# Six more landing places for the first weights, one modulation run per block, and three changes of order in a two-layer diffusion kernel

## The chip, the cores and the metric

The kernel runs on one core of a Trainium2 chip. The metric is the device time of one execution in microseconds (us), lower is better. TensorE is called PE here, VectorE DVE, ScalarE ACT, GpSimd POOL and SyncE SP; "PEld" is the loading of a matmul's stationary operand, which overlaps PE.

## The reference

Everything is float32: 256 latent tokens and 256 context tokens of width 2048, batch 1, two layers.

```
for i in range(2):
    shift, scale, gate = split(silu(c) @ ada_w[i] + ada_b[i], 3)
    h = rms_norm(x, norm_g[i]) * (1 + scale) + shift
    if i == 0:                                  # attention heads beside a state-space scan
        hc = the same of ctx, with the modulation vector c_ctx
        p, pc = h @ w_in, hc @ w_in             # q, gate, z, k, v, x/B/C, dt
        ya = neighbourhood_attention(norm(q), norm(k), v, norm(kc), vc, rpb) * silu(gate)
        yb = group_norm(bidirectional_ssd(conv(x,B,C), dt, ctx state) + d*x, silu(z))
        y = concat(ya, yb) @ w_out
    else:                                       # gated short convolution
        bg, cg, hv, g = split(h @ w_in, 4)
        y = (silu(g) * bg * conv3(cg * hv)) @ w_out
    x = x + gate * y
```

## The kernel before, in words

**Matmuls.** Each matrix product is made of three matmuls. A weight block of 128 x 1024 numbers arrives by DMA in a buffer called `raw`; ACT casts it to a rounded format (`wH`, line 414), DVE subtracts to get the remainder (`wL`, line 421), and the activations are split in the same way into `hH` (line 742) and `hL` (line 748). PE then sums hH·wH, hL·wH and hH·wL in a PSUM bank. Every such matmul is issued by the helper at line 189, every transposition by the one at line 193. There are eight PSUM banks, five `raw` buffers and three places for a split weight (`WH`, `WL`). Four tiles that have no work yet at the start (`PT0`, `PT1`, `xtm`, `yi`) serve as further `raw` buffers until `later_loads` takes them back.

**The first stage.** The first 160 us or so go through the 2048 input channels in eight blocks of 256, because the normalised input becomes ready block by block. In each block j, `ada_gen` computes scale (A0) and shift (S0) of the block for the latent and the context stream at once: 16 matmuls for each of the two parts, each using 32 of the 128 columns of the array (operand `cpad`), an ACT copy of the result (`half`, line 712), two transpositions and a short DVE reduction (lines 720 to 726). Then ACT and DVE make `hH` and `hL` of the two 128-channel halves. The main loop over j multiplies the block by the weights of K and V (four row groups t of 128 tokens, six matmuls each, each into a bank of its own, which DVE then adds into a running sum in SBUF, line 774: `sz` and `gt` hold K, `Vt` holds V), by those of Q (two row groups, in two fixed banks) and by a narrow block for the state-space part (`b_part`, two fixed banks). So four banks are left to turn over among the K and V parts and the modulation.

**Order.** The instruction order of all engines is written out by a planner at build time. `Plan` keeps a clock for each engine, with a cost for each instruction and a DMA rate (`RATE`). Tasks are generators that yield the engine and the operands that they wait for; `pump` lets a task issue when the planner's clocks say that it would not wait long, `force` issues whatever can go first until a condition holds. `urgent`, `side` and `back` are three queues of tasks in falling priority. On the chip each engine runs its list in order, so an instruction that waits holds back all behind it on its engine. The loads of weights go out on SP in one list, each when a buffer has become free.

```
def used():
    pos["use"] += 1
    free_w.append(in_use.popleft())
    splits_try()
```

A weight's place is given back by `used`, and then the next landed weight may be cast into it. In block one, K, V and Q are held together and given back after the last row group.

**Later stages.** Attention heads and state-space groups run as side tasks beside the remaining projections of the first layer. The vectors that gate the two residuals are a matrix-vector product on DVE (`gemv_gen`, line 802), spread in the background over all that time, fed by loads of `in_ada_w`. In the last projection of V (`v_gen`, line 996) two of the four copies out of PSUM go to DVE and two to ACT. The matmuls with `mix` that follow are the first layer's output projection; then come the second layer's input and output projections. The last one writes four column groups n; for each, `fin_gen` multiplies both halves of rows by the gate (line 1945), adds the residual (line 1947) and sends the result out (line 1949). Within a weight chunk the two halves of rows t alternate.

Of the kernel before, what the change touches and what calls it, by code (L numbers as in the profile page):

```python
# [9 lines left out]
F32R = mybir.dt.float32r  # L10
# [27 lines left out]
class Plan:  # L38


    NAMES = {"PE": "PE", "DVE": "DVE", "Activation": "ACT", "Pool": "POOL", "SP": "SP"}
    RATE = 270.0

    def __init__(self):
        self.t = dict.fromkeys(("PE", "DVE", "ACT", "POOL", "SP"), 0.0)
# [4 lines left out]
    def keys(self, ap):  # L50
        a, n = ap.ap, ap.tensor.name
        if type(ap.tensor).__name__ == "Tile" and not n.startswith("dram"):
            lo = ap.offset % a[0][0] if a[0][0] else ap.offset
            hi = lo + sum(abs(s) * (c - 1) for s, c in a[1:])
            return [(n, u) for u in range(lo // 128, hi // 128 + 1)]
        if n.startswith("in_") or n.startswith("out_"):
            return []
        hi = ap.offset + sum(abs(s) * (c - 1) for s, c in a)
        return [(n, u) for u in range(ap.offset // 256, hi // 256 + 1)]
# [82 lines left out]
def kernel(ctx: ExitStack, tc, x, cx, ada0, ada_w, ada_b, w_in, w_out, sc_in, sc_out, rpb, small, const,  # L142
# [12 lines left out]
    def st(shape, tag, dt=F32, name=None):  # L155
        return sb.tile(list(shape), dt, tag=tag, name=name or tag, bufs=1)
# [10 lines left out]
    WH = [st([128, 1024], f"wH{k}", F32R) for k in range(NW)]  # L167
    WL = [st([128, 1024], f"wL{k}", F32R) for k in range(NW)]

    KT, QT, Vt, gt = st([128, 4, 512], "KT", F32R), st([128, 4, 256], "QT", F32R), st([128, 4, 512], "Vt"), st([128, 4, 256], "gt")  # L170
    KL, QL = st([128, 4, 512], "KL", F32R), st([128, 4, 256], "QL", F32R)
    sz, xtm, yi = st([128, 4, 256], "sz"), st([128, 2, 512], "xtm"), st([128, 4, 256], "yi")
    PT = [st([128, 4, 256], f"PT{k}") for k in range(2)]

    spare = [t.rearrange("p a b -> p (a b)") for t in (PT[0], PT[1], xtm, yi)]
    free_r += spare
    spare_names = {t.tensor.name for t in spare}

# [151 lines left out]
    def bank():  # L330
        return take(free_b)
# [138 lines left out]

    def used():
        pos["use"] += 1
        free_w.append(in_use.popleft())
        splits_try()


# [16 lines left out]

    def later_loads():
        started[0] = True
        free_r[:] = [a for a in free_r if a.tensor.name not in spare_names]
        for n in range(16):
            lay = 0 if n < 4 else 1
            c0 = 4096 + n * 512 if n < 4 else (n - 4) * 512
            for k in range(8):  # L500
                later.append(("g", ("gem", n, k), ada_w[lay], k * 256, 2, c0, 512))
# [183 lines left out]

    A0 = st([128, KB, 2], "A0")
    S0 = st([128, KB, 2], "S0")
    g0 = P_("g0")

    def ada_gen():  # L690
        bc = lambda ap: ap.unsqueeze(2).to_broadcast([128, 2, 2])
        for j in range(8):
            k2 = slice(2 * j, 2 * j + 2)
            for part, dst in ((0, A0), (1, S0)):
                ps = None
                for q in range(4):
                    key = ("ada", j, part, q)
                    w_ = 2 if j == 0 else 4
                    if q % w_ == 0:
                        ks = [("ada", j, part, q + i) for i in range(w_)]  # L700
                        yield when(lambda: all(k in RAW for k in ks))
                        yield W_("PE", *[RAW[k][1] for k in ks], nb=0 if ps is not None else 1)
                    if ps is None:
                        ps = bank()
                    raw, v = RAW.pop(key)
                    for g in range(4):
                        mm(ps[32 * g:32 * g + 32, :256], cpad[:, 4 * q + g, :], v[:, g, :], q == 0, q == 3)
                    give_raw(raw)
                    issue()
                yield W_("ACT", ps)  # L710
                Rt = half()
                E(S.copy(Rt, ps[:, :256]))

                yield W_("PE", Rt)
                for b in range(2):
                    turn(ps[:, 256 + b * 128:384 + b * 128], Rt[:, b * 128:(b + 1) * 128])
                give(free_h, Rt)
                yield W_("DVE", ps)
                p2 = dst[:, k2, :]
                E(V.tensor_reduce(out=p2, in_=ps[:, 256:].rearrange("p (b g c) -> p b c g", b=2, c=32)[:, :, 0:2, :],  # L720
                                  axis=AX.X, op=ALU.add))
                if part == 0:
                    E(V.tensor_tensor(out=dst[:, k2, :], in0=p2, in1=bc(bs1[:, k2]), op=ALU.add))
                    E(V.tensor_tensor(out=dst[:, k2, :], in0=dst[:, k2, :], in1=bc(g0[:, k2]), op=ALU.mult))
                else:
                    E(V.tensor_tensor(out=dst[:, k2, :], in0=p2, in1=bc(P_("ab0")[:, k2]), op=ALU.add))
                give(free_b, ps)

            for ts in ((0, 1), (2,), (3,)) if j == 0 else ((0, 1, 2, 3),):
                yield when(lambda: all(("xm", t, j) in got for t in ts))  # L730
                spans = [(k, slice(max(256 * k, 128 * ts[0]), min(256 * k + 256, 128 * ts[-1] + 128)))
                         for k in range(2) if {2 * k, 2 * k + 1} & set(ts)]
                o = slice(128 * ts[0], 128 * ts[-1] + 128)
                for kb in (2 * j, 2 * j + 1):
                    yield W_("DVE", xnT[kb][:, o])
                    hf = tmp()
                    if hH[kb] is None:
                        hH[kb] = st([128, 512], f"hH{kb}", F32R, name=f"hH{kb}")
                    if ts == (0, 1):
                        split_half(kb)  # L740
                    for k, ok_ in spans:
                        E(S.activation(hH[kb][:, ok_], xnT[kb][:, ok_], AF.Identity, scale=A0[:, kb, k:k + 1],  # L742
                                       bias=S0[:, kb, k:k + 1]))
                        E(V.tensor_scalar(out=hf[:, ok_], in0=xnT[kb][:, ok_], scalar1=A0[:, kb, k:k + 1],  # L744
                                          scalar2=S0[:, kb, k:k + 1], op0=ALU.mult, op1=ALU.add))
                    if hL[kb] is None:
                        hL[kb] = st([128, 512], f"hL{kb}", F32R, name=f"hL{kb}")
                    E(V.tensor_tensor(out=hL[kb][:, o], in0=hf[:, o], in1=hH[kb][:, o].bitcast(F32), op=ALU.subtract))  # L748
                    give(free_t, hf)
                    if ts == (0, 1):  # L750
                        halfsplit.pop()()
                if ts == (0, 1):
                    hold[0] = False
                    split()
                    split()
                got.update(("h", j, t) for t in ts)
# [102 lines left out]
        used()  # L859

    for j in range(8):
        force(lambda: ("h", j, 0 if j == 0 else 3) in got, (urgent,))
        if j == 0:

# [14 lines left out]
                rows_(j, "Q", t, psQ[t], w3[2], True, False)  # L879
            for t in range(2, 4):  # L880
                force(lambda: ("h", j, t) in got, (urgent,))
                for key, k in (("K", 0), ("V", 1)):
                    kv(j, key, t, w3[k])
            for k in range(3):
# [3 lines left out]
        else:  # L888
# [7 lines left out]
                used()  # L896
            b_part(j)
    force(lambda: all(("part", 7, key, t) in got for key in "KV" for t in range(4)), (urgent,))
    got.add(("V", 0))


# [615 lines left out]
    def do_gv(a, nxt):  # L1517
        do_g(a, 4)
        psV = banks(4)
        proj(512, "act", psV, nxt, a == 3)  # L1520
        spawn(urgent, v_gen(a, psV))

    for a in range(1, 3):
        do_qk(a, 2)
# [410 lines left out]
    def fin_gen(n, ps):  # L1935
        cols = slice(n * 512, (n + 1) * 512)
        yield when(lambda: n_back[0] >= 15)
        gb, o = tmp(), tmp()
        yield W_("SP", mrow[3:4])
        E(DMA.dma_start(gb, mrow[3, cols].partition_broadcast(128)))  # L1940
        for t in range(2):
            if t:
                o = tmp()
            yield W_("DVE", ps[t], gb)
            E(V.tensor_tensor(out=o, in0=ps[t], in1=gb, op=ALU.mult))
            give(free_b, ps[t])
            E(V.tensor_tensor(out=o, in0=o, in1=x1[t][:, cols], op=ALU.add))
            yield W_("SP", o)
            E(DMA.dma_start(out[t * 128:(t + 1) * 128, cols], o))
            give(free_t, o)  # L1950
        give(free_t, gb)

    for n in range(4):
        if n == 1:
            force(lambda: n_back[0] >= 15, (urgent, back))
        ps = banks(2)
        for kb in range(0, KB, 2):
            force(lambda: y2[kb + 1] is not None)
            chunk(kb, "act", ps, kb == 0, kb == KB - 2, lambda i: (y2[i][:, 0], y2[i][:, 1]))
        spawn(urgent, fin_gen(n, ps), 3)  # L1960
    force(lambda: not urgent, (urgent,))


# [54 lines left out]
```

## Time and profile before

| | before |
|---|---|
| median of 3 runs (lowest to highest) | 1783.97 us (1783.84 to 1785.52) |
| the profiled execution's own time | 1784.02 us |
| its span in the profile | 1782.2 us |
| PE busy | 1755.5 us (99%), 9577 records |
| DVE / ACT / POOL busy | 71% / 43% / 2% of the span |
| mean DMA rate | 210 GB/s |

The profiled execution took 1784.02 us, of which 1.8 us lie outside the span. Matmuls are pipelined, so a matmul's busy time runs into the next one's; how fast PE issues is seen from the starts of neighbouring rows. PE's clock was granted in full throughout.

### The profile page before, as it was taken

How to read it: one execution, taken by the hardware profiler on the slowest of the kernel's cores; microseconds unless marked ns; L12 is line 12 of the kernel's file. 1: busy time of each engine (PE TensorE's matmuls, PEld its weight loads, DVE VectorE, ACT ScalarE, POOL GpSimd, SP SyncE). 2: the span in 40 equal slices, each digit the busy share in tenths (PEclk: the TensorE clock that was granted, in tenths of full speed). 3: DMA queues.
4: the chain of work that ended last, by engine and by line, in shares of the span. 5: the costliest groups of instructions: out<-in, count | busy, mean ns of one | idle time of the engine just before them, and what ended most of it. 6: DMA issues, size and time to landing. Idle time of an engine off the chain costs nothing.

```text
span 1782.2 us, 25428 instructions
## 1 busy us (share of the span) xinstructions
PE 1755.5 (99%) x9577; PEld 1470.5 (83%) x9577; DVE 1265.6 (71%) x1986; ACT 773.7 (43%) x1330; POOL 32.2 (2%) x28
## 2 busy tenths in 40 slices
PE   6999999999999999999999999999999999999998
PEld 4677888888888889888988898788888888888887
DVE  5666787878675878675887687787768777555554
ACT  5423544445242446242445443664546444444432
POOL 0000100001000000000001000000000000000000
PEclk9999999999999999999999999999999999999999
DMA  9987654666745666655675457658867787666563
GB/s 354 345 284 246 213 153 130 192 193 209 226 132 186 199 193 206 208 153 172 187 233 141 149 178 249 208 166 293 283 225 248 241 260 251 208 190 190 191 209 116
DMA packets 222363, 374.60 MB, mean 210 GB/s; under 512 B 32432, under 2 KB 69136, under 8 KB 222240
## 3 DMA queue, kind: packets, MB, share of 16 engines
q1 hardware_dynamic: 214928, 366.38, 63.9%
q10 hardware_dynamic: 7312, 6.61, 1.1%
q8 instruction: 75, 1.23, 0.3%
q14 instruction: 48, 0.39, 0.1%
HBM read 367.52 MB, written 6.72 MB: 210 GB/s over the span
## 4 chain that ended last, share of the span: by engine, by line
PE 93%; DMA 3%; DVE 2%; ACT 1%; issue 0%; POOL 0%; SPq 0%; ACTq 0%; DVEq 0%
PE bank L189 90%; PE bank L193 3%; DMA tmp<-dram_csr 1%; DVE wL L421 1%; DMA raw<-in_ada 0%; DMA tmp<-dram_exr 0%; DVE mix L1546 0%; DMA tmp<-dram_mixd 0%; DMA const<-in_const 0%; ACT wH L414 0%; DVE tmp L744 0%; DMA raw<-in_w_out 0%; DVE tmp L1388 0%; DVE hL L748 0%; DVE tmp L1399 0%
## 5 line engine op out<-in xcount | busy, mean ns | idle before, releaser
L414 ACT CAST wH<-raw 128x1024 fp32r<-128x1024 f32 (+1 forms) x375 | 390.8, 1044 | 595.0 <-PE bank L189 515.9
L421 DVE TENSOR_TENSOR wL<-raw,wH 128x1024 fp32r<-128x1024 f32 (+1 forms) x374 | 452.2, 1212 | 214.3 <-ACT wH L414 212.4
L189 PE MATMUL bank<-hH,wH 128*128 128x256 f32 (+1 forms) x1040 | 343.3, 330 | 0.8 <-ACT wH L414 0.8
L189 PE MATMUL bank<-hL,wH 128*128 128x256 f32 (+1 forms) x1040 | 338.0, 325 | 0.0
L189 PE MATMUL bank<-hH,wL 128*128 128x256 f32 (+1 forms) x1024 | 330.7, 323 | 0.9 <-DVE wL L421 0.9
L189 PE MATMUL bank<-wH,hH 128*128 128x512 f32 x640 | 257.1, 402 | 3.9 <-ACT hH L742 2.6
L189 PE MATMUL bank<-wL,hH 128*128 128x512 f32 x640 | 250.4, 392 | 0.0
L189 PE MATMUL bank<-wH,hL 128*128 128x512 f32 x640 | 249.8, 391 | 0.1
L802 DVE SCALAR_TENSOR_TENSOR acc<-raw,csil,acc 128x512 f32<-128x512 f32 x256 | 191.8, 749 | 65.2 <-DMA raw<-in_ada_w 56.0
L189 PE MATMUL bank<-wH,h 128*128 128x512 f32 x680 | 215.6, 391 | 0.0
L189 PEld LDWEIGHTS bank<-hH,wH 128*128 128x128 f32 x1040 | 196.5, 189 | 18.6 <-ACT wH L414 1.3
L189 PEld LDWEIGHTS bank<-hL,wH 128*128 128x128 f32 x1040 | 196.8, 189 | 15.5
L189 PEld LDWEIGHTS bank<-hH,wL 128*128 128x128 f32 x1024 | 194.0, 189 | 18.2 <-DVE wL L421 1.6
L189 PEld LDWEIGHTS bank<-wH,h 128*128 128x128 f32 x680 | 127.7, 188 | 26.5 <-issue 0.2
L189 PEld LDWEIGHTS bank<-wH,hH 128*128 128x128 f32 x640 | 120.2, 188 | 33.7 <-issue 5.0
L189 PEld LDWEIGHTS bank<-wH,hL 128*128 128x128 f32 x640 | 120.2, 188 | 26.1 <-DVE hL L748 0.6
L189 PEld LDWEIGHTS bank<-wL,hH 128*128 128x128 f32 x640 | 120.2, 188 | 24.7 <-DVE wL L437 0.5
L189 PE MATMUL bank<-wH,mix 128*128 128x512 f32 x432 | 138.8, 393 | 1.1 <-DVE Vt L996 1.1
L189 PE MATMUL bank<-wL,h 128*128 128x512 f32 x340 | 132.3, 389 | 0.0
L189 PEld LDWEIGHTS bank<-wH,mix 128*128 128x128 f32 x432 | 81.1, 188 | 18.7 <-DVE Vt L996 1.5
L189 PE MATMUL bank<-wL,mix 128*128 128x512 f32 x216 | 84.4, 391 | 0.3 <-DVE wL L421 0.3
L189 PEld LDWEIGHTS bank<-wL,h 128*128 128x128 f32 x340 | 63.9, 188 | 12.9
(284 smaller groups left out, 2173.9 us busy)
## 6 DMA issues: line engine op xcount, KB each, us to landing
raw<-in_w_in SPq DMA_DIRECT2D x208, 512.0 KB
raw<-in_ada_w SPq DMA_DIRECT2D x128, 512.0 KB
raw<-in_sc_in SPq DMA_DIRECT2D x128, 512.0 KB
raw<-in_w_out SPq DMA_DIRECT2D x64, 512.0 KB
raw<-in_ada SPq DMA_DIRECT2D x37, 512.0 KB
raw<-in_sc_out SPq DMA_DIRECT2D x32, 512.0 KB
tmp<-dram_csr SPq DMA_DIRECT2D x32, 256.0 KB
PT<-in_ada SPq DMA_DIRECT2D x14, 512.0 KB
```

Of the source, the lines that this page charges most:

```text
L189: E(T.matmul(o, l, r, start=start, stop=stop, skip_group_check=True))
L193: E(T.transpose(o, i, ident if k == 128 else ident[:k, :k]))
L414: E(S.copy(H, v))
L421: E(V.tensor_tensor(out=Lo, in0=v, in1=H.bitcast(F32), op=ALU.subtract))
L802: E(V.scalar_tensor_tensor(out=acc, in0=v[:, j], scalar=csil[:, 2 * k + j:2 * k + j + 1], in1=acc, op0=ALU.mult, op1=ALU.add))
```

## The change

The instructions that compute weights' products stay the same. The change has these parts:

1. QT, QL, KT and KL, which are written only after the first stage, lend their space: six more `raw` places until `later_loads`. Their real tiles are allocated after the stage.
2. For blocks four to eight (j > 2) scale and shift are computed in one run: 32 matmuls into one bank, one ACT copy of 128 x 512, four transpositions, one reduction of 128 x 8 into AS, three small operations.
3. For those blocks the making of `hH`/`hL` waits, for each half, until the main loop has reached the block or the planner's DVE clock is at most 600 ns ahead of PE's.
4. In block one Q's place is given back when only the last row group of K and V is left, so that the next weight is cast there earlier.
5. `v_gen` goes to the front of the urgent queue.
6. In the last column group the last six 128-channel blocks are done for the first half of rows, then for the second, and `fin_gen` waits for each half's marker before it takes that half's bank.
7. The planner: RATE is 310 in the first stage and 270 from `later_loads` on, and dependences on `small` and `const` are kept at a granularity of 2 columns instead of 128. These change no instruction, only the order that the planner chooses.

```
-    RATE = 270.0
+    RATE = 310.0
...
+            g = 2 if n[:5] in ("small", "const") else 128
+            return [(n, u) for u in range(lo // g, hi // g + 1)]
...
-    spare = [t.rearrange("p a b -> p (a b)") for t in (PT[0], PT[1], xtm, yi)]
+    spare = [t.rearrange("p a b -> p (a b)") for t in (PT[0], PT[1], xtm, yi)] + \
+        [st([128, 1024], n, name=f"first{n}") for n in ("QT", "QL")]
+    for n in ("KT", "KL"):
+        kt = st([128, 2, 1024], n, name=f"first{n}")
+        spare += [kt[:, 0], kt[:, 1]]
...
+        w = in_use.popleft()
+        if w is not None:
+            free_w.append(w)
...
     def later_loads():
         started[0] = True
+        plan.RATE = 270.0
...
+            if j > 2:
+                ks = [("ada", j, part, q) for part in range(2) for q in range(4)]
+                yield when(lambda: all(k in RAW for k in ks))
+                yield W_("PE", *[RAW[k][1] for k in ks], nb=1)
+                ps = bank()
+                for _, _, part, q in ks:
+                    raw, v = RAW.pop(("ada", j, part, q))
                     for g in range(4):
+                        mm(ps[32 * g:32 * g + 32, part * 256:part * 256 + 256], cpad[:, 4 * q + g, :], v[:, g, :],
+                           q == 0 and part == 0, q == 3)
...
+                Rt = tmp()
+                E(S.copy(Rt, ps))
...
+                for b in range(4):
+                    turn(ps[:, b * 128:(b + 1) * 128], Rt[:, b * 128:(b + 1) * 128])
...
+                E(V.tensor_reduce(out=AS, in_=ps.rearrange("p (b g c) -> p b c g", b=4, c=32)[:, :, 0:2, :], axis=AX.X, op=ALU.add))
+                E(V.tensor_tensor(out=A0[:, k2, :], in0=AS[:, 0:2], in1=bc(bs1[:, k2]), op=ALU.add))
+                E(V.tensor_tensor(out=A0[:, k2, :], in0=A0[:, k2, :], in1=bc(g0[:, k2]), op=ALU.mult))
+                E(V.tensor_tensor(out=S0[:, k2, :], in0=AS[:, 2:4], in1=bc(P_("ab0")[:, k2]), op=ALU.add))
...
                 for kb in (2 * j, 2 * j + 1):
+                    if j > 2:
+                        yield when(lambda: need[0] >= j or plan.t["DVE"] <= plan.t["PE"] + 600)
...
     for j in range(8):
+        need[0] = j
...
                 force(lambda: ("h", j, t) in got, (urgent,))
+                if t == 3:
+                    free_w.append(in_use[2])
+                    in_use[2] = None
+                    splits_try()
...
-        spawn(urgent, v_gen(a, psV))
+        urgent.insert(0, Task(v_gen(a, psV)))
...
+            yield when(lambda: n < 3 or (3, t) in at)
             yield W_("DVE", ps[t], gb)
             E(V.tensor_tensor(out=o, in0=ps[t], in1=gb, op=ALU.mult))
...
-        for kb in range(0, KB, 2):
+        for kb in range(0, KB if n < 3 else KB - 6, 2):
...
+    ws = [use(q) for q in range(3)]
+    for t in range(2):
+        for q, (H, Lo) in enumerate(ws):
+            for b in range(2):
+                hl = y2[KB - 6 + 2 * q + b]
+                for a_, w_ in ((0, H), (0, Lo), (1, H)):
+                    mm(ps[t], hl[:, a_, t * 128:(t + 1) * 128], w_[:, b], False, q == 2 and b == 1 and a_ == 1)
+                pump()
+        at.append((3, t))
+        pump()
```

More of the change, by code (lines that the diff above doesn't have):

```diff
@@ L54, in keys @@
             hi = lo + sum(abs(s) * (c - 1) for s, c in a[1:])
-            return [(n, u) for u in range(lo // 128, hi // 128 + 1)]
+            g = 2 if n[:5] in ("small", "const") else 128
+            return [(n, u) for u in range(lo // g, hi // g + 1)]
         if n.startswith("in_") or n.startswith("out_"):
@@ L168 @@
     WL = [st([128, 1024], f"wL{k}", F32R) for k in range(NW)]
-    KT, QT, Vt, gt = st([128, 4, 512], "KT", F32R), st([128, 4, 256], "QT", F32R), st([128, 4, 512], "Vt"), st([128, 4, 256], "gt")
-    KL, QL = st([128, 4, 512], "KL", F32R), st([128, 4, 256], "QL", F32R)
+    Vt, gt = st([128, 4, 512], "Vt"), st([128, 4, 256], "gt")
     sz, xtm, yi = st([128, 4, 256], "sz"), st([128, 2, 512], "xtm"), st([128, 4, 256], "yi")
     PT = [st([128, 4, 256], f"PT{k}") for k in range(2)]
-    spare = [t.rearrange("p a b -> p (a b)") for t in (PT[0], PT[1], xtm, yi)]
+    spare = [t.rearrange("p a b -> p (a b)") for t in (PT[0], PT[1], xtm, yi)] + \
[3 more added lines that the diff above has]
+        spare += [kt[:, 0], kt[:, 1]]
     free_r += spare
@@ L472, in used @@
         pos["use"] += 1
-        free_w.append(in_use.popleft())
+        w = in_use.popleft()
+        if w is not None:
+            free_w.append(w)
         splits_try()
@@ L687 @@
     S0 = st([128, KB, 2], "S0")
+    AS = st([128, 4, 2], "AS")
     g0 = P_("g0")
+    need = [0]
     def ada_gen():
@@ L693, in ada_gen @@
             k2 = slice(2 * j, 2 * j + 2)
[L694 to L705, printed above, removed]
+            if j > 2:
[5 more added lines that the diff above has]
+                    raw, v = RAW.pop(("ada", j, part, q))
                     for g in range(4):
-                        mm(ps[32 * g:32 * g + 32, :256], cpad[:, 4 * q + g, :], v[:, g, :], q == 0, q == 3)
+                        mm(ps[32 * g:32 * g + 32, part * 256:part * 256 + 256], cpad[:, 4 * q + g, :], v[:, g, :],
+                           q == 0 and part == 0, q == 3)
                     give_raw(raw)
@@ L710, in ada_gen @@
                 yield W_("ACT", ps)
-                Rt = half()
-                E(S.copy(Rt, ps[:, :256]))
+                Rt = tmp()
+                E(S.copy(Rt, ps))
                 yield W_("PE", Rt)
-                for b in range(2):
-                    turn(ps[:, 256 + b * 128:384 + b * 128], Rt[:, b * 128:(b + 1) * 128])
-                give(free_h, Rt)
+                for b in range(4):
+                    turn(ps[:, b * 128:(b + 1) * 128], Rt[:, b * 128:(b + 1) * 128])
+                give(free_t, Rt)
@@ L718, in ada_gen @@
                 yield W_("DVE", ps)
[L719 to L726, printed above, removed]
@@ L727, in ada_gen @@
-                give(free_b, ps)
+                E(V.tensor_reduce(out=AS, in_=ps.rearrange("p (b g c) -> p b c g", b=4, c=32)[:, :, 0:2, :], axis=AX.X, op=ALU.add))
+                E(V.tensor_tensor(out=A0[:, k2, :], in0=AS[:, 0:2], in1=bc(bs1[:, k2]), op=ALU.add))
+                E(V.tensor_tensor(out=A0[:, k2, :], in0=A0[:, k2, :], in1=bc(g0[:, k2]), op=ALU.mult))
+                E(V.tensor_tensor(out=S0[:, k2, :], in0=AS[:, 2:4], in1=bc(P_("ab0")[:, k2]), op=ALU.add))
+                give(free_b, ps)
+            else:
+                for part, dst in ((0, A0), (1, S0)):
+                    ps = None
+                    for q in range(4):
+                        key = ("ada", j, part, q)
+                        w_ = 4 if j else 2
+                        if q % w_ == 0:
+                            ks = [("ada", j, part, q + i) for i in range(w_)]
+                            yield when(lambda: all(k in RAW for k in ks))
+                            yield W_("PE", *[RAW[k][1] for k in ks], nb=0 if ps is not None else 1)
+                        if ps is None:
+                            ps = bank()
+                        raw, v = RAW.pop(key)
+                        for g in range(4):
+                            mm(ps[32 * g:32 * g + 32, :256], cpad[:, 4 * q + g, :], v[:, g, :], q == 0, q == 3)
+                        give_raw(raw)
+                        issue()
+                    yield W_("ACT", ps)
+                    Rt = half()
+                    E(S.copy(Rt, ps[:, :256]))
+                    yield W_("PE", Rt)
+                    for b in range(2):
+                        turn(ps[:, 256 + b * 128:384 + b * 128], Rt[:, b * 128:(b + 1) * 128])
+                    give(free_h, Rt)
+                    yield W_("DVE", ps)
+                    p2 = dst[:, k2, :]
+                    E(V.tensor_reduce(out=p2, in_=ps[:, 256:].rearrange("p (b g c) -> p b c g", b=2, c=32)[:, :, 0:2, :],
+                                      axis=AX.X, op=ALU.add))
+                    if part == 0:
+                        E(V.tensor_tensor(out=dst[:, k2, :], in0=p2, in1=bc(bs1[:, k2]), op=ALU.add))
+                        E(V.tensor_tensor(out=dst[:, k2, :], in0=dst[:, k2, :], in1=bc(g0[:, k2]), op=ALU.mult))
+                    else:
+                        E(V.tensor_tensor(out=dst[:, k2, :], in0=p2, in1=bc(P_("ab0")[:, k2]), op=ALU.add))
+                    give(free_b, ps)
@@ L898 @@
     force(lambda: all(("part", 7, key, t) in got for key in "KV" for t in range(4)), (urgent,))
+    KT, QT, KL, QL = st([128, 4, 512], "KT", F32R), st([128, 4, 256], "QT", F32R), st([128, 4, 512], "KL", F32R), st([128, 4, 256], "QL", F32R)
     got.add(("V", 0))
@@ L1960 @@
         spawn(urgent, fin_gen(n, ps), 3)
+    ws = [use(q) for q in range(3)]
+    for t in range(2):
+        for q, (H, Lo) in enumerate(ws):
+            for b in range(2):
+                hl = y2[KB - 6 + 2 * q + b]
[4 more added lines that the diff above has]
+        pump()
     force(lambda: not urgent, (urgent,))
```

## The prediction, on record before the changed kernel ran

> **What bounds the kernel now.** I read the page's busy line and the chain's shares first, then the list of what PE waited for, to see how much there is to win at all.
>
> ```profile
> span 1782.2 us, 25428 instructions
> PE 1755.5 (99%) x9577; PEld 1470.5 (83%) x9577; DVE 1265.6 (71%) x1986; ACT 773.7 (43%) x1330; POOL 32.2 (2%) x28
> PE 93%; DMA 3%; DVE 2%; ACT 1%; issue 0%; POOL 0%; SPq 0%; ACTq 0%; DVEq 0%
> PE bank L189 <- DMA raw<-in_ada: 11.9, 1, 11.9
> PE bank L189 <- ACT hH L742: 2.6, 2, 1.4
> PE bank L189 <- DVE wL L421: 1.2, 3, 0.7
> PE bank L189 <- DVE Vt L996: 1.1, 1, 1.1
> PE bank L189 <- DVE sz L774: 1.0, 1, 1.0
> PE bank L193 <- ACT half L712: 1.0, 2, 0.5
> PE bank L189 <- ACT wH L414: 0.8, 1, 0.8
> PE bank L189 <- DVE half L1433: 0.5, 1, 0.5
> PE bank L189 <- DVE tmp L1404: 0.4, 1, 0.4
> ```
>
> The columns of the last nine rows are the total wait in us, how often, and the longest. PE is busy for 99% of the span and carries 93% of the chain that ended last. The nine rows sum to 20.5 us, of which 11.9 is the one wait for the first loads, which nothing in the change shortens. So all waits that the change could remove come to 8.6 us, and everything that DVE or ACT saves counts only where it stands in one of these rows. What else can be won is PE's own work (the modulation runs) and the tail behind the last matmul. I make the sum against the profiled execution's own time, 1784.02 us (span 1782.2 and 1.8 around it), which is 0.05 above the median, so the same sum holds for the median. A measurement of this kernel can tell about 0.2%, 3.57 us, from no change.
>
> **The change part by part.**
>
> One modulation run for scale and shift, five blocks. This is one of the runs of a later block, on PE's timeline (start, duration, operation):
>
> ```profile
> 79.03 0.39 PE L189 MATMUL bank<-wL,hH 128*128 128x512 f32 x1
> 79.35 1.07 PE L189 MATMUL bank<-raw,cpad 128*32 128x256 f32 x16
> 80.24 1.05 PE L189 MATMUL bank<-PT,cpad 128*32 128x256 f32 x16
> 81.22 0.50 PE L189 MATMUL bank<-wH,hH 128*128 128x512 f32 x1
> 81.55 0.39 PE L189 MATMUL bank<-wH,hL 128*128 128x512 f32 x1
> 82.01 0.38 PE L193 MATMUL bank<-const,half 128*128 128x128 f32 x2
> 82.15 0.48 PE L189 MATMUL bank<-wH,hH 128*128 128x512 f32 x1
> 82.46 0.39 PE L189 MATMUL bank<-wH,hL 128*128 128x512 f32 x1
> ```
>
> A plain 128x512 matmul follows its neighbour by 0.23 (82.69 would be next after 82.46; 81.55 + 2 x 0.23 is 82.01). Each of the program's matmuls with `cpad` stands as two records, so the 16 of one part are these 32, in two halves of 0.89 (79.35 to 80.24) and 0.98 to the next operation. From 79.03 to 81.55 there are 2.52, of which two plain steps are 0.46: one part's run costs 2.06. Entering and leaving the 32-column form is 2.06 - 2 x 0.89 = 0.28 of that. A merged run has four halves and pays this once: 3.84 instead of 4.12, so 0.28 less in each of five blocks: **-1.4**. The transpositions: a pair takes 82.46 - 82.01 - 0.23 = 0.22, two pairs 0.44; four in a row cost between 0.22 and 0.44, so the gain is 0 to 0.22 per block; I take 0, the upper price, because each transposition still has its own issue (all five: 0 to -1.1). ACT makes one copy of 512 columns instead of two of 256 and DVE three small operations fewer in a block; PE waits for neither there (the wait for `half` line 712, 1.0 in all, is two of 0.5, in the first block, which keeps two runs): 0. A merged run starts when eight landed blocks lie in their places instead of four; nine places would be tight for that, and part 1 makes them fifteen. If it came late or its bank was held too long, that goes to "other".
>
> The waits of the first stage that parts 1, 3, 4 and 7 move. The last column in brackets is PE's idle time and who ended it.
>
> ```profile
> 51.10 0.50 PE L189 MATMUL bank<-hH,wH 128*128 128x512 f32 x1 [0.83 <-ACT wH L414]
> 52.09 0.50 PE L189 MATMUL bank<-hH,wL 128*128 128x512 f32 x1 [0.26 <-DVE wL L421]
> 67.72 0.68 DVE L421 TENSOR_TENSOR wL<-PT,wH 128x512 fp32r<-128x512 f32 x1
> 67.86 0.50 PE L189 MATMUL bank<-wH,hH 128*128 128x512 f32 x1 [0.34 <-DVE gt L774]
> 86.16 0.40 PE L189 MATMUL bank<-wL,hH 128*128 128x512 f32 x1
> 87.56 0.50 PE L189 MATMUL bank<-wH,hH 128*128 128x512 f32 x1 [1.00 <-DVE sz L774]
> ```
>
> At 87.56 PE starts 87.56 - 86.16 - 0.23 = 1.17 late, because the adds that free K's banks stood on DVE behind the making of a later block's `hH` and `hL`. That is what the gate of part 3 moves behind: **-1.1** (0 to -1.17). Nothing is queued on an engine behind the gate, but the next block's modulation is in the same task and comes later too; what is late next is a block's own `hH`, which PE met twice in this trace, with 2.6 in all and 1.4 at most. The gate opens when the block is reached at the latest; a wait of that size once is among "other" below.
>
> At 67.86 the work is that of block three (j = 2), which is not gated. In the changed order the bank's add stands behind one more `wL` half of 0.68 (row 67.72): **+0.2** (-0.5 to +0.7).
>
> At 51.10 and 52.09 block one's next weight waits for a place; part 4 gives Q's place back one row group sooner. But the cast then meets two casts of `hH` on ACT and its remainder the queue on DVE, so the same weight is still the last thing to come, and in the changed order it is K's weight of block two: **0** (-1.1, both rows and nothing new, to +0.3).
>
> Six more places. They let SP issue loads earlier, so what matters is whether the DMA engines had room. The windows' last three columns are PE's clock, DMA's busy share and GB/s:
>
> ```profile
> 8.00:36.00 28.00, 20.46 (x139) 14.05 (x139) 16.96 (x44) 17.62 (x39) 1.55 (x3) 1.00 1.03 397
> 12.00:16.00 4.00, 3.88 (x25) 2.19 (x22) 1.26 (x3) 1.71 (x3) 0.24 (x1) 1.00 1.03 419
> 40.00:44.00 4.00, 4.00 (x58) 2.56 (x60) 2.47 (x9) 2.50 (x8) 0.00 (x0) 1.00 0.70 232
> ```
>
> From 8 to 36 us, the only stretch where PE is short of data, the queues are full (share 1.03) with the nine places there are; more requests outstanding add nothing to that. Only at 40 to 44 is there room (0.70, 232 GB/s), and there PE is busy for 4.00 of 4.00. The order of the bytes on SP's list stays. So: **0** by itself (-1.5 to +0.5; the lower end is rival C). The Trainium skill, "Perfetto Trace Analysis", Engine Utilization, puts the 16 DMA engines at about 435 GB/s in aggregate as one core's ceiling; as an estimate from that figure the stretch at 397 would have 28 x (1 - 397/435) = 2.4 us in it and the sum would be 2.4 lower. No row of this trace reaches that; the best one has 419.
>
> Behind the first stage the same list of work is issued with its order moved slightly.
>
> ```profile
> 205.89 0.75 DVE L802 SCALAR_TENSOR_TENSOR acc<-raw,csil,acc 128x512 f32<-128x512 f32 x1 [4.13 <-DMA raw<-in_ada_w]
> 208.62 0.39 PE L189 MATMUL bank<-hH,wL 128*128 128x256 f32 x1 [0.66 <-DVE wL L421]
> 1140.41 0.50 PE L189 MATMUL bank<-wH,mix 128*128 128x512 f32 x1 [1.11 <-DVE Vt L996]
> ```
>
> At 208.62 PE waits for a `wL` that came late because DVE stood 4.13 at the gate vector's load. With the loads running earlier this pair no longer stands there: **-0.6** (0 to -0.66). At 1140.41 the bank is freed by V's copy (line 996); part 5 puts this copy ahead of the other urgent work: **-1.0** (0 to -1.11). Of what part 5 moves back, the state-space tasks, none is in the list of waits with more than 0.5 us.
>
> The tail.
>
> ```profile
> 1776.40 0.69 DVE L1945 TENSOR_TENSOR tmp<-bank,tmp 128x512 f32<-128x512 f32 x1 [13.39 <-PE bank L189]
> 1776.66 0.39 PE L189 MATMUL bank<-wH,y 128*128 128x512 f32 x1
> 1777.13 0.69 DVE L1947 TENSOR_TENSOR tmp<-tmp,x1a 128x512 f32<-128x512 f32 x1
> 1777.74 0.68 DVE L1945 TENSOR_TENSOR tmp<-bank,tmp 128x512 f32<-128x512 f32 x1
> 1778.46 0.69 DVE L1947 TENSOR_TENSOR tmp<-tmp,x1b 128x512 f32<-128x512 f32 x1
> ```
>
> Now both halves end together and four DVE operations follow in a row, to 1778.46 + 0.69 = 1779.15. With the first half ended 18 matmuls sooner, its two lie beside PE. The second half's first can start at 1776.66 + 0.39 = 1777.05, its second 0.72 later, ending at 1778.46: **-0.7** (-0.5 to -0.8). The last output then goes out alone, as now.
>
> New waits that the moved order makes elsewhere: I cannot see them in a trace of before. Their size is that of the single waits listed, 0.4 to 1.4; none to three of them, and I take **+0.4** (0 to +3).
>
> Sum: -1.4 + 0 - 1.1 + 0.2 + 0 + 0 - 0.6 - 1.0 - 0.7 + 0.4 = -4.2, so **1779.8 us**. With all hidden gains, 1.1 for the transpositions, 1.1 for Q's place, and no new wait it is 1777.2; with the two waits of DVE (1.1 and 1.0) only half gone and one more new one of 0.6 it is 1781.5. That is the forecast's own range.
>
> **The rivals.**
>
> A: the moved order gives back what it wins. Waits of 0.3 to 1.4 turn up at other places as fast as the listed ones go; only the merged runs and the tail, which need no luck, remain: 1784.0 - 1.4 - 0.7 = 1781.9, within 0.2%. For it: each of the listed waits is under 1.5 us and depends on the position of one DVE operation. Against: the changed lists keep PE's order nearly, and DVE has 29% of the span free. That the parts would do nothing at all is excluded for these two, since the merged runs and the last six blocks' order stand in PE's list.
>
> B: slower. The gate vectors' loads start earlier, and in the changed DVE list six pairs of line 802 stand before the last part sums of the first stage, the first of them in front of three V sums of an earlier block.
>
> ```profile
> DVE acc L802 <- DMA raw<-in_ada_w: 56.0, 44, 4.1
> L802 DVE SCALAR_TENSOR_TENSOR acc<-raw,csil,acc x14: 746/752/753, 169.8 to 206.7; 128x512 f32<-128x512 f32 x14
> ```
>
> DVE waits 44 times for such a load, up to 4.1, and whatever stands behind it, a sum that frees a bank, waits too. A K or V part of six matmuls is 6 x 0.23 = 1.4 of PE's work, so with two banks in hand PE bears 2.7; beyond that it stops. If each of the six pairs waited 4.13, that is 1.4 each, 8.4 in all: 1779.8 + 8.4 = 1788.2. Against: the mean wait is 56.0 / 44 = 1.3, below 2.7, and the 14 additions from 169.8 to 206.7 in the trace stop for the load just once.
>
> C: the loads come sooner. If more outstanding requests brought 8 to 36 us to the best row's 419 GB/s, 28 x (1 - 397/419) = 1.5 would go from the start: 1778.3. Against it stands the full share of 1.03.
>
> **How the numbers follow.** Forecast 0.65, A 0.18, B 0.12, C 0.05. The bound of faster by over 0.2% lies at 1780.4, 0.6 above my number; of the forecast's 0.65 I put 0.10 above it. Faster: 0.55 + 0.05 = 0.60. Same: 0.10 + 0.18 = 0.28. Slower: 0.12. The range goes from 1776.0 (the 1777.2 above, with most of C's 1.5) to 1785.0, which takes in A with three new waits of 1; B stays out above.
>
> **What would show it.** Right: in five blocks one row of 64 `cpad` records with 3.8 between its neighbours; no wait of 1.00 for K's sum near 87 us; no 1.1 at the first output projection; two DVE operations after the last matmul, not four. PE's list of waits without the first load below 8.6. Wrong: PE waits of over 1 us for a sum or a `wL` at 130 to 200 us, with DVE standing at a gate vector's load (B), a first stage that ends over 1 us sooner than merged runs and the gate explain (C), or new rows in the list of waits that sum to over 2 us (A).

## The result, and the profile after

The changed kernel takes 1790.04 us (median of 8 runs, 1788.11 to 1795.54) against 1784.15 us for the kernel before beside it: a ratio of 1.0035, 95% interval 1.0023 to 1.0047. It is slower by about 6 us; 4 us faster had been forecast. The profiled execution took 1788.11 us, 4.1 more than that of before.

The page of the changed kernel (span, busy time, chain):

```profile
span 1786.3 us, 25369 instructions
PE 1762.1 (99%) x9577; PEld 1472.2 (82%) x9577; DVE 1265.2 (71%) x1981; ACT 773.1 (43%) x1325; POOL 33.5 (2%) x28
PE 93%; DMA 4%; DVE 2%; ACT 1%; issue 0%; SPq 0%; POOL 0%; DVEq 0%; ACTq 0%
```

Its list of what PE waited for (total us, times, longest), down to 0.5:

```profile
PE bank L193 <- DMA raw<-in_ada: 11.8, 1, 11.8
PE bank L193 <- ACT hH L783: 2.6, 2, 1.4
PE bank L193 <- DVE tmp L1452: 1.5, 1, 1.5
PE bank L197 <- ACT half L750: 1.0, 2, 0.5
PE bank L193 <- DVE gt L815: 0.9, 1, 0.9
PE bank L193 <- DVE half L1481: 0.7, 2, 0.4
PE bank L193 <- DVE wL L425: 0.5, 1, 0.5
```

This is the puzzle: PE waits less than before (these rows sum to 19.0 us, those of before to 20.5; the waits for `sz`, `Vt` and `wH` are gone), it has the same number of matmuls, and its busy time rose from 1755.5 to 1762.1 us. Something made the matmuls themselves slower, and the list of waits cannot show that. The starts of equal rows on PE's timeline can. Here is the last output projection of before, one row for each group of three matmuls (two with `wH`, one with `wL`, all 512 wide); the rows left out hold the other matmuls.

```profile
1760.05 0.39 PE L189 MATMUL bank<-wL,y 128*128 128x512 f32 x1
...
1766.23 0.39 PE L189 MATMUL bank<-wL,y 128*128 128x512 f32 x1
...
1774.39 0.39 PE L189 MATMUL bank<-wL,y 128*128 128x512 f32 x1
...
1776.43 0.39 PE L189 MATMUL bank<-wL,y 128*128 128x512 f32 x1
```

From 1760.05 to 1766.23 are nine groups: 0.687 us each. From 1774.39 to 1776.43 are three: 0.680. The same code in the same stage has two paces. In the changed kernel only the slower one is left (nine groups of 0.687, and three more at the very end):

```profile
1762.61 0.39 PE L193 MATMUL bank<-wL,y 128*128 128x512 f32 x1
...
1768.79 0.39 PE L193 MATMUL bank<-wL,y 128*128 128x512 f32 x1
...
1779.09 0.39 PE L193 MATMUL bank<-QL,y 128*128 128x512 f32 x1
...
1781.15 0.39 PE L193 MATMUL bank<-wL,y 128*128 128x512 f32 x1
```

What differs between the two paces of before is the channel block, and with it the tile `y2` that is loaded as the stationary operand. I set each matmul's starts beside the addresses that the built programs give its operands (bytes within a partition). In before, `y2`, `mix` and `hH` of the first eight 128-channel blocks begin 64 past a multiple of 128, all others at a multiple (in every kernel here that is 128 past a multiple of 256). In the changed kernel all sixteen begin at 64, and `hL`, `mix` and `h1` of two blocks at 32. The changed order of the loads does it: with six more places the first round of loads runs further down its list, so the tiles of the last eight blocks (`xs`, whose space `hH`, `mix` and `y2` take over) are allocated before the 64-byte tile `bs1` and no longer after it; and the 32-byte tile `AS` of part 2 moves two `hL` tiles. Medians over both traces, in ns for a group of three 512-wide matmuls, all of whose steps (from one start to the next) are shorter than 255 ns (number of groups in before, in the changed kernel). With `hH` two of the three read `hH` and one `hL`; `hL` begins at a multiple in these rows:

```
operand                start past a multiple of 128    ns
stationary y, h, mix    0                             680   (739, 546)
stationary y, mix      64                             687   (116, 241)
stationary h, mix      32                             699   (-, 73)
stationary hH           0                             680   (288, -)
stationary hH          64                             689   (256, 482)
moving hH               0                             680   (185, -)
moving hH              64                      699 to 700   (169, 324)
```

Summed over all 512-wide steps shorter than 255 ns, the mean step goes from 228.47 to 229.81 ns, which is +7.6 us for some 5700 of them. The rest of the 4.1 us between the two profiled executions, from PE's start-to-start times: modulation runs -2.2, tail -0.7, first matmul -0.1, a stretch at half clock +1.4 (below), waits and everything else -2.0.

The half clock is in the windows (PE's granted clock is third from the end) of the changed kernel:

```profile
24.00:28.00 4.00, 3.78 (x11) 2.74 (x12) 3.69 (x7) 4.00 (x8) 0.00 (x0) 0.68 1.04 382
28.00:32.00 4.00, 4.00 (x17) 3.24 (x16) 3.70 (x10) 2.67 (x7) 0.55 (x1) 0.89 1.06 386
```

Seven steps from 25.3 to 28.7 us took 0.43 instead of 0.23. The clock lost in the two rows, 4 x (1 - 0.68) + 4 x (1 - 0.89) = 1.7 us, is a stretch of 3.4 us at half clock. Which of the two orders a kernel has does not decide it: of the experiments below, number 3, with the order of before, has it (first row), and number 1, with the order of the changed kernel, has not (second row).

```profile
24.00:28.00 4.00, 4.00 (x11) 2.90 (x12) 3.90 (x7) 3.95 (x8) 0.00 (x0) 0.64 1.04 385
```

```profile
24.00:28.00 4.00, 3.20 (x13) 2.25 (x14) 3.58 (x8) 3.85 (x6) 0.00 (x0) 1.00 1.05 387
```

The Trainium skill, "TensorE: Matmul & The Clock Gate", Part 1, describes a free-running activity window of about 3.4 us after which the PE clock is halved or restored, so that the same kernel can meet it or miss it; the stretch of 3.4 us and its coming in some executions only agree with that here.

How often it comes is not settled. The mean granted clock was 0.998 or lower in six of the changed kernel's eight executions, in one of the 34 of the kernel before that ran beside the experiments, and in two of the twelve of experiments 1 and 7, which are one program. A clock lower by 0.001 is 1.8 us over this span, so some 2 of the 6 us between the two medians may be clock and not addresses. Why the changed kernel met it more often was not tested.

### The profile page after: what moved, and what is told of

It is laid out like the page before. It is cut to its first block, busy times and chain, and to the rows that moved or that the text cites. A ratio compares the mean times of both kernels' runs of the same rounds, so it can differ in the third digit from the quotient of the medians.

```text
span 1786.3 us, 25369 instructions
## 1 busy us (share of the span) xinstructions
PE 1762.1 (99%) x9577; PEld 1472.2 (82%) x9577; DVE 1265.2 (71%) x1981; ACT 773.1 (43%) x1325; POOL 33.5 (2%) x28
## 4 chain that ended last, share of the span: by engine, by line
PE 93%; DMA 4%; DVE 2%; ACT 1%; issue 0%; SPq 0%; POOL 0%; DVEq 0%; ACTq 0%
PE bank L193 90%; PE bank L197 3%; DMA tmp<-dram_csr 1%; DMA PT<-in_w_in 1%; DMA PT<-in_ada 1%; DVE wL L425 1%; DMA firstKT<-in_ada 0%; DMA xs<-in_cx 0%; ACT wH L418 0%; DMA firstKL<-in_ada 0%; DMA xs<-in_x 0%; DMA raw<-in_ada_w 0%; DMA small<-in_small 0%; ACT tmp L1442 0%; DVE tmp L1447 0%
## 5 line engine op out<-in xcount | busy, mean ns | idle before, releaser
L418 ACT CAST wH<-raw 128x1024 fp32r<-128x1024 f32 (+1 forms) x361 | 379.0, 1050 | 583.8 <-PE bank L193 507.1
L425 DVE TENSOR_TENSOR wL<-raw,wH 128x1024 fp32r<-128x1024 f32 (+1 forms) x360 | 438.8, 1221 | 244.3 <-ACT wH L418 242.4
```

Of the source, the lines that this page charges most:

```text
L418: E(S.copy(H, v))
L425: E(V.tensor_tensor(out=Lo, in0=v, in1=H.bitcast(F32), op=ALU.subtract))
```

## The experiments

Theory: the start addresses of the matmuls' operands cost the time. Rivals: the clock or chance of the executions; waits moved by the new order.

**1. The changed kernel with all operands at multiples of 128.**

```
     ssq = st([128, 16], "ssq")
+    bs1 = st([128, 16], "bs1")
...
-    bs1 = st([128, 16], "bs1")
...
-    AS = st([128, 4, 2], "AS")
+    AS = None
...
+                if AS is None:
+                    AS = st([128, 4, 2], "AS")
```

> The changed kernel with two small tiles allocated at another moment (bs1 beside ssq, AS at block four), so that every operand of the 128x512 matmuls starts at a multiple of 128 bytes; instruction order unchanged. Theory (start addresses): in the changed kernel's trace a group of three matmuls with a stationary block takes 680 ns at a multiple of 128, 687 at 64 past it, 698 at 32 past it, and three with hH moving 680 or 699. 2048 stationary blocks at 64 x 2.2 ns + 320 at 32 x 6 + 784 moving at 64 x 9.5 = 13.8 us go: 1790.0 - 13.8 = about 1776, faster than before by about 8. Rival (the slower cadence is the chip's clock or chance of the execution, not the addresses): 1790, as the changed kernel. Second rival (moved waits cost the time): 1790 too.

The second part allocates `AS` at block four, behind the `hL` tiles of the first blocks.

Measured: 1776.77 us, ratio to before 0.9955 (0.9942 to 0.9968). That is the theory's number, 13 us below the changed kernel with the same instruction order on every engine. In the two traces the 512-wide steps became 13.7 us shorter, as expected. That the total fits as well has some luck in it: the stretch at half clock is missing here (-1.4), and the 256-wide steps became 2.2 us longer (last section). Its last projection has only the faster pace, 14 groups in 9.52 us, 0.680 each:

```profile
1750.19 0.39 PE L193 MATMUL bank<-wL,y 128*128 128x512 f32 x1
...
1759.71 0.39 PE L193 MATMUL bank<-wL,y 128*128 128x512 f32 x1
```

The moving operand shows in the groups of the 512-wide matmuls with `hH` moving (total us, mean ns of one): before, changed, and this kernel.

```profile
L189 PE MATMUL bank<-hH,wH 128*128 128x512 f32 x400 | 160.1, 400 | 0.8 <-ACT wH L414 0.8
```

```profile
L193 PE MATMUL bank<-hH,wH 128*128 128x512 f32 x400 | 160.5, 401 | 0.0
```

```profile
L193 PE MATMUL bank<-hH,wH 128*128 128x512 f32 x400 | 157.9, 395 | 0.0
```

**2. The kernel before, aligned.** Only `bs1` moves, as above; no instruction changes its place.

> The kernel before with bs1 allocated beside ssq, nothing else: the first eight hH, mix and y2 tiles move from 64 past a multiple of 128 bytes to a multiple. Start addresses: 1024 stationary x 2.2 ns + 392 moving x 9.5 = 5.9 us go: about 1778. Rivals: 1784, no change.

Measured: 1778.66 us, ratio 0.9972 (0.9961 to 0.9983). One moved allocation of 64 bytes is worth 0.28%. (Its profiled execution, 1788.03 us, is the slowest of its twelve, with a mean granted clock of 0.997; its waits are not used here.)

**3. The kernel before with the changed kernel's offsets.**

```
+            if t == 2 and q == 0:
+                r2s.extend(st([128, 2], f"r2_{k}") for k in range(2))
             xt = st([128, 512], f"hH{4 * t + q}", name=f"xs{4 * t + q}")
...
+            if t == 3 and q == 3:
+                s4s.extend(st([128, 8], f"s4_{k}") for k in range(3))
```

> The kernel before with five small tiles (r2, s4) allocated earlier, so that its operands start at exactly the changed kernel's offsets (2048 stationary at 64, 320 at 32, 784 moving at 64 instead of 1024, 0, 392); instruction order that of before. Start addresses: 13.8 - 5.9 = 7.9 us more: about 1792. Rivals: 1784.

Measured: 1795.19 us, ratio 1.0053 (1.0041 to 1.0065). The order of before and none of the parts of the change, and it is slower still. It is 3 us over the expected 1792, and its trace shows a reason: the offsets match only modulo 128. Its second eight tiles start 192 past a multiple of 256, where those of the changed kernel start 64 past one. A group with such a `y` or `mix` tile stationary took 700 ns (median of 122) and not 687, one with `hH` stationary 694 (288) and not 689. For 384 and 640 matmuls that is, as an estimate, 384 x 13 / 3 + 640 x 5 / 2 ns = 3.3 us more.

**4. Six more places alone** (part 1 of the change in the kernel before).

```
-    spare = [t.rearrange("p a b -> p (a b)") for t in (PT[0], PT[1], xtm, yi)]
+    spare = [t.rearrange("p a b -> p (a b)") for t in (PT[0], PT[1], xtm, yi)] + \
+        [st([128, 1024], n, name=f"first{n}") for n in ("QT", "QL")]
+    for n in ("KT", "KL"):
+        kt = st([128, 2, 1024], n, name=f"first{n}")
+        spare += [kt[:, 0], kt[:, 1]]
...
```

> The kernel before with part 1 alone (six more places). The loads of the last eight xs tiles go out before bs1 is allocated, so all sixteen hH, mix and y2 tiles start 64 past a multiple of 128 (2048 stationary, 784 moving), hL stays. Start addresses: 4.5 + 7.4 - 5.9 = 6.0 us more than before, about 1790, and if the halved clock near 26 us comes from the earlier start, one or two us more. Rival (places alone do nothing, as the prediction had it): 1784.

Measured: 1795.14 us, ratio 1.0057 (1.0045 to 1.0069), 5 more than the addresses explain. On PE's timeline the transpositions of the first x rows come late:

```profile
26.67 0.69 PE L196 MATMUL bank<-const,xs 128*128 128x128 f32 x2 [3.87 <-ACT xs L606]
```

The order of this kernel puts more of the modulation ahead of these rows; that the planner's DMA rate, still at 270, is the reason was not tested. Behind the wait PE ran at half clock for a while (its granted clock is 0.79 from 24 to 32 us). In the whole change the first K group starts at 24.22 us, here at 33.09.

**8. The same, aligned** (`bs1` beside `ssq`).

> The kernel of experiment 4 (before with six more places) with bs1 allocated beside ssq, so that all operands start at multiples of 128 bytes. Start addresses: 2048 x 2.2 + 784 x 9.5 = 11.9 us less than experiment 4's 1795.1, about 1783. What is left over experiment 2's 1778.7, about 4.5, would be the order: in experiment 4 PE waits 4.1 us for the first normalised x rows near 26 us and starts the first K block 7.8 us later. Rival (places alone cost nothing but addresses): 1779.

Measured: 1786.7 us, ratio 1.0013 (1.0003 to 1.0022). The addresses gave 8 to 9 us back, not 11.9: the 512-wide steps became 12 us shorter, as expected, but the 256-wide ones 2.5 longer (last section). Against experiment 2, where the addresses are in place too, the six places cost about 0.4%, 7 us, so this is the cost of the order that they bring. About 4 of it is the wait for the x rows, which stands in this list of waits too. Another part is clock: its ten executions had 0.996 to 0.998, on average 0.9973, against 0.9991 in experiment 2, which over the span is 3 us.

```profile
PE bank L196 <- ACT xs L606: 4.3, 3, 3.9
```

**5. The dose: 32 instead of 0.** Experiment 2 with `rx` (32 bytes) allocated ahead of the activations.

```
     bs1 = st([128, 16], "bs1")
+    rx = st([128, 4], "rx")
...
-    rx = st([128, 4], "rx")
```

> The kernel of experiment 2 (before, aligned) with one 32-byte tile (rx) allocated ahead of the activations: 3264 stationary blocks and 742 moving operands of the 512-wide matmuls start 32 past a multiple of 128 bytes, instruction order unchanged. Start addresses, dose: 3264 x 6 ns = 19.6 us more than experiment 2's 1778.7, and 0 to 7 more for the moving ones (742 x 0 to 9.5 ns, not measured at 32 yet): 1798 to 1806. Rival (only an offset of 64, or only the tiles' place among DVE and ACT traffic matters): 1779 to 1785.

Measured: 1802.94 us, ratio 1.0108 (1.0095 to 1.0122), in the expected range. One tile that takes 32 bytes costs 24 us against experiment 2. Its last projection has both paces again, now with a larger step: eight groups of 0.700 with the eight tiles at 32, then 0.680 with those at a multiple of 128.

```profile
1777.71 0.40 PE L189 MATMUL bank<-wL,y 128*128 128x512 f32 x1
...
1783.31 0.40 PE L189 MATMUL bank<-wL,y 128*128 128x512 f32 x1
...
1794.27 0.39 PE L189 MATMUL bank<-wL,y 128*128 128x512 f32 x1
...
1796.31 0.39 PE L189 MATMUL bank<-wL,y 128*128 128x512 f32 x1
```

**6. Part 2 undone, aligned.** Experiment 1 with scale and shift of every block in two runs (the branch is taken for no block).

> The kernel of experiment 1 (changed, aligned) with part 2 undone: every block computes scale and shift in two runs as before; the rest of the change stays. The prediction's term: 1.4 more than experiment 1's 1776.8, 1778.2; by the steps into and out of the 32-column matmuls in the traces (12.85 to 9.8 us, 0.86 more inside) 2.2 more, 1779. Rival (the merged run only moved a wait): 1776.8.

Measured: 1774.87 us, ratio 0.9951 (0.9939 to 0.9964), no slower than experiment 1, and the lowest median of all kernels, though the intervals overlap. The merged runs do save time where they stand: near the end of the first stage the same matmul starts at 164.69 us in experiment 1 and at 166.03 here, whose first matmul was 0.33 earlier, so 1.7 (against the second trace of experiment 1's program, below, 1.2). In the whole time this saving is not to be seen. One state-space wait near 396 us goes the other way (1.6 in experiment 1's list of waits), which this kernel's list does not have:

```profile
PE bank L193 <- DVE tmp L1454: 1.6, 1, 1.6
```

```profile
PE bank L193 <- DMA raw<-in_ada: 11.4, 1, 11.4
PE bank L193 <- ACT hH L785: 2.6, 2, 1.4
PE bank L197 <- ACT half L752: 1.0, 2, 0.5
PE bank L193 <- DVE gt L817: 1.0, 1, 1.0
PE bank L193 <- DVE wL L425: 0.5, 1, 0.5
PE bank L193 <- DVE half L1483: 0.4, 1, 0.4
```

**7. Part 5 undone, aligned** (`spawn(urgent, v_gen(a, psV))` again).

> The kernel of experiment 1 with part 5 undone: V's copies go to the end of the urgent queue. The prediction's term: the wait near 1140 us returns, 1.0 to 1.8 more. Rival: part 5 also made the state-space wait near 396 us longer (1.86 us against 0.70 before), which now shrinks by 1.1, so 0 to 0.7 more in all.

Measured: 1778.43 us, ratio 0.9972 (0.9961 to 0.9983). This run cannot tell what part 5 is worth, because the edit alters nothing: the program built from it is the same as that of experiment 1, instruction for instruction, and so are the operations in the two traces. The planner issues V's copies at the same place from the end of the queue as from its front. No wait could return near 1140 us, and none did.

What the run does show is how far seven more executions of one program can lie from the first five: 1.7 us by the medians, 3.0 by the ratios. Its trace has three state-space waits, 4.4 us in all (list of waits), where experiment 1's trace has one of 1.6. The longer of the two new ones is near 668 us (timeline), and a stretch at half clock stands behind it (granted clock 0.72 from 668 to 674 us):

```profile
PE bank L193 <- DVE tmp L1454: 4.4, 3, 2.1
```

```profile
668.67 0.54 PE L193 MATMUL bank<-tmp,xtm 128*64 128x128 f32 x5 [1.97 <-DVE tmp L1454]
```

So a wait of 1 to 2 us in a single trace need not come from the order of the instructions, and a difference of 2 to 3 us between two kernels is not settled by these runs.

## Why the prediction was wrong

**The step that failed is the one with no term.** The sum took a plain 128x512 matmul at 0.23 us before and after, and put the six more places at 0 "by itself", looking only at the DMA engines. They moved eight more blocks of `hH`, `mix` and `y2` to 64 past a multiple of 128, and part 2's small tile `AS` moved two blocks of `hL`, `mix` and `h1` to 32 past one. With them went the pace of the matmuls that read them: +7.6 us in the profiled execution, of which, by the prices in the expectations, about 6 belong to the places (1024 x 2.2 + 392 x 9.5 ns) and 2 to `AS` (320 x 6 ns). No rival had it either; all three were about waits or loads. Experiments 1 to 3 show that the addresses are the cause, in both orders and both directions, with no instruction of either order changed.

**The signs came true all the same.** Everything that the prediction named as a sign of being right is in the profile: the runs of 64 records, no wait of 1.00 near 87 us, no 1.1 at the first output projection, two DVE operations at the end, and 7.2 us of waits without the first load, below 8.6. All of them watch waits and the order of work. None watches the pace of a matmul, so they could not tell a faster kernel from a slower one.

**Merged runs, -1.4.** Right in place. One run on PE's timeline of the changed kernel, and its transpositions:

```profile
95.67 0.39 PE L193 MATMUL bank<-hH,wL 128*128 128x512 f32 x1
95.98 1.93 PE L193 MATMUL bank<-raw,cpad 128*32 128x256 f32 x32
97.73 1.05 PE L193 MATMUL bank<-PT,cpad 128*32 128x256 f32 x16
98.60 0.61 PE L193 MATMUL bank<-xtm,cpad 128*32 128x256 f32 x8
99.03 0.61 PE L193 MATMUL bank<-yi,cpad 128*32 128x256 f32 x8
99.57 0.50 PE L193 MATMUL bank<-hH,wH 128*128 128x512 f32 x1
99.91 0.39 PE L193 MATMUL bank<-hL,wH 128*128 128x512 f32 x1
101.07 0.60 PE L197 MATMUL bank<-const,tmp 128*128 128x128 f32 x4
101.43 0.48 PE L193 MATMUL bank<-wH,hH 128*128 128x512 f32 x1
101.75 0.40 PE L193 MATMUL bank<-wH,hL 128*128 128x512 f32 x1
```

The 64 records cost 99.91 - 95.67 - 0.46 = 3.78 (forecast 3.84), the four transpositions 101.75 - 101.07 - 0.23 = 0.45 (0.44). Over the whole kernel undoing it costs nothing that the runs can show (experiment 6).

**Gate, -1.1.** The wait for K's sum near 87 us is gone: no `sz` row is left. The gate was not undone alone, so that it is the reason is argued, not shown.

**Third block, +0.2, and Q's place, 0.** Both waits, as brackets on PE's timeline:

```profile
54.48 0.50 PE L193 MATMUL bank<-wL,hH 128*128 128x512 f32 x1 [0.53 <-DVE wL L425]
69.48 0.50 PE L193 MATMUL bank<-wH,hH 128*128 128x512 f32 x1 [0.91 <-DVE gt L815]
```

The second grew from 0.34 to 0.91, +0.6, in the stated bounds. (Its work is that of block two and not of block three: the stationary tile is `hH2`, and block j has `hH` number 2j and 2j + 1. Neither block is gated.) The first replaces 0.83 and 0.26, so Q's place was worth 0.5 and not 0; the new wait is a `wL`, as forecast.

**The waits at 208.62 and 1140.41, -0.6 and -1.0.** Both are gone. For the second the reason was wrong: part 5 alters no instruction (experiment 7), so another part of the new order, not singled out here, removed it.

**Tail, -0.7.** Two operations behind the last matmul, not four:

```profile
1781.38 0.40 PE L193 MATMUL bank<-wH,y 128*128 128x512 f32 x1
1781.81 0.69 DVE L1995 TENSOR_TENSOR tmp<-bank,tmp 128x512 f32<-128x512 f32 x1 [2.71 <-PE bank L193]
1782.54 0.69 DVE L1997 TENSOR_TENSOR tmp<-tmp,x1b 128x512 f32<-128x512 f32 x1
```

From the last matmul's start to the span's end it is 4.9 us instead of 5.6.

**New waits, +0.4.** The largest is the state-space wait, from 0.4 to 1.5, +1.1.

**The rivals.** B did not happen: no wait of PE lies between 130 and 200 us. C neither: the first K group starts 1.05 us sooner, but this is lost again by 40 us, to the half clock (1.4): the six transpositions that begin at 39.51 in before begin at 39.77. With the addresses out of the way the change is worth little. Experiment 1 lies 1.9 us below experiment 2 by the medians and 3.0 by the ratios, experiment 7, the same program, 0.2 by the medians and 0 by the ratios. So the forecast's 4.2 was too high for the terms that it did have, A's 2.1 would fit, and these runs cannot tell it from nothing.

## What to carry to other kernels

When a change allocates, reorders or resizes tiles, compare the operands' start addresses of the matmuls before and after, and the spacing of equal matmul rows in an unchanged stage: a pace that differs by 1 to 3% shows in no list of waits, and here it outweighed all the stalls that the change removed. In this kernel it paid to put small tiles where they add up to a multiple of 128 bytes, or behind the large ones. The gain of removing a wait is best checked by undoing that part alone. Compare the built programs first, to see that the part does anything at all, and time one program twice, to see how small a gain can be told.

## What the runs showed of the hardware

Matmuls with 512 columns on operands in the rounded fp32 format were slower when an operand began off a multiple of 128 bytes in its partition: a group of three took 680 ns at a multiple, 687 with `y` or `mix` stationary from 64 past a multiple of 256, 700 from 192, 699 to 700 from 32, and 699 to 700 with `hH` moving from 64. All the multiples of 128 in these kernels are 128 past a multiple of 256; a multiple of 256 was not tried. The address is not all that counts: the 26 to 28 groups of the attention scores (`KT` or `KL` moving, `QT` or `QL` stationary), at multiples in every kernel, took 680 to 698. The Trainium skill, "SBUF — State Buffer", section Operand start alignment, asks only for a multiple of the element size and says that it is about legality and not speed; these runs put a price on speed. What in the read path makes it is open. The 256-wide matmuls with `hH` moving went the other way: a group took 356 ns from 64 and 360 from a multiple of 128, and the mean 256-wide step rose from 118.3 ns in experiment 4 to 119.5 in experiment 8, which is 2.5 us over some 2075 steps.
